# Weight tiles 64 bytes wider in a two-layer decoder trunk: six starts within 512 bytes

## The chip, the cores and the metric

The kernel runs on one core of a Trainium2 chip. The metric is the device time of one execution in microseconds (us). TensorE (PE in the profile; PEld is its weight load) multiplies matrices, VectorE (DVE), ScalarE (ACT) and GpSimd (POOL) do elementwise work, and SyncE (SP) issues nearly all DMA transfers.

## The reference

A sequence of 512 tokens with 1024 channels passes two layers in float32. Each layer is a mixer and a gated MLP, both with a residual sum and an RMSNorm ahead of them:

```
h = rmsnorm(x, norm_mix_e[e])
x = x + conv_mla_mixer(h, ...)      # layer 0: convolution branch + latent attention
h = rmsnorm(x, norm_mix_o[o])
x = x + pool_mixer(h, ...)          # layer 1: trailing means over 2, 4, 8, 16 tokens
...
h = rmsnorm(x, norm_ffn[l])         # both layers
uv = h @ w_up[l]                    # 1024 -> 2 x 2816
x = x + (silu(causal_dwconv(u)) * v) @ w_down[l]     # 2816 -> 1024
```

Layer 0's mixer projects h once; half of the columns go through a gated causal convolution of width 31 with a LayerNorm, the other part through attention with 8 heads and low-rank queries, keys and values. The output has a final RMSNorm. Nearly all arithmetic is in the projections, above all in the two MLPs.

## The kernel before

All activations are kept transposed: channels lie on the 128 partitions, the 512 tokens along the free dimension, in 8 tiles of 128 channels. A projection is a sum over such tiles, 128 channels at a time, into one bank of PSUM.

**Three matmuls for one product.** To keep float32 accuracy, each operand is split into a high and a low part of the type f32r, and a product is three matmuls: high x high, high x low and low x high. `mm3` (L107) issues them: L108 has the high weights and the high activations, L109 the high weights and the low activations, L110 the low weights and the high activations. The first operand of a matmul is the stationary one, which a weight load brings into TensorE; the second one streams past it. With few exceptions the weights are stationary, 128 x 128 at a time, and 512 tokens stream. In the profile's names the streaming operand comes first: `ps<-xgh,hi` streams the high activations against the high weights. The moving tiles are called xgh and xgl (inputs of a projection), gh and gl (the gated product in the MLP, bands and pooled values in the pooling mixer) and s (latents and attention). In two places the weights stream instead: the values of the attention (L580) and the pooling mixer's projection (L839).

**Weight tiles.** `stream` (L130) lists all weights in the order of their use, mostly in pieces of 128 x 1024, 4096 bytes on each partition. `fetch` (L146) brings one into a raw tile by a DMA that SP issues. `prepare` (L152) takes a high and a low tile and calls `split` (L96): ScalarE copies raw into hi (L97, rounding to f32r), VectorE writes raw - hi into lo (L98). `weights` (L164) hands the next pair out and prepares one ahead. There are three buffers each of raw, hi and lo, all from the pool `p_w`; a new hi waits until TensorE has done with the tile of three pieces ago. A weight tile holds eight blocks of 128 x 128, 512 bytes on a partition each, which `part` (L123) cuts out.

**Some matmuls are in plain f32**, of which the prediction speaks: 16 taps of the convolution (L392: 512 columns of u from offset j against a diagonal matrix), the scores (L511), the transposes (L546), probabilities times values (L558) and the sums of squares (L239). Each shows as two records in the profile.

**Where tiles lie.** Pools take their place one behind the other along the partition, consts, resid, `p_w`, `p_t` (temporaries), `p_s`, then the mixer's tiles or the MLP's gates from the left; the xg tiles lie at the far end, on the right side. Three unused tiles of `W_PAD`, `T_PAD` and `R_PAD` columns (4 bytes each) shift what follows them (L41, L143, L175, L273). The allocation of the built program gives these starts:

| tiles | start, bytes past a multiple of 512 |
|---|---|
| raw (3), hi (3), lo (3) | 0, each |
| xgh, xgl, gh, gl, s, u, q, keys, pt, v, tap | 0, each |
| t (8) | 96, 128, 160, 192, 224, 256, 288, 320 |
| sqr, rows, d | 352 |
| x, sq (ones, identity), causal | 320 |

Around the weight tiles no order is written by hand: each engine's instructions follow the program text, with waits where a tile's reader or writer is on another engine. The weight tiles' code is this, with what calls it:

Of the kernel before, what the change touches and what calls it, by code (L numbers as in the profile page):

```python
# [9 lines left out]
F32R = mybir.dt.float32r  # L10
# [5 lines left out]
P = 128  # L16
# [21 lines left out]

WARM = 40
PE_TAPS = 16  # L40
W_PAD, T_PAD, R_PAD = 48, 16, 120  # L41
GLU, LAT, BLK, END = 3, 4, 2, 0


# [1 line left out]
def kernel(  # L46
# [24 lines left out]
    p_w = ctx.enter_context(tc.tile_pool(name="weights", bufs=3))  # L71
# [7 lines left out]
    def uid(s):  # L79
        count[0] += 1  # L80
        return f"{s}{count[0]}"
# [14 lines left out]
    def split(dst, src):  # L96
        i = act.copy(dst[0], src)  # L97
        dve.tensor_tensor(dst[1], src, dst[0].bitcast(F32), op=ALU.subtract)  # L98
        return i
# [46 lines left out]
    def fetch():  # L146
        src, n = stream[len(raws)]
        raw = p_w.tile([P, 1024], F32, tag="raw", name=uid("raw"))[:, :n]
        nc.sync.dma_start(raw, src)
        raws.append(raw)  # L150

    def prepare():  # L152
        i = len(ready)
        if i == len(raws):
            fetch()
        n = stream[i][1]
        hi = p_w.tile([P, 1024], F32R, tag="hi", name=uid("hi"))[:, :n]
        lo = p_w.tile([P, 1024], F32R, tag="lo", name=uid("lo"))[:, :n]
        copied = split((hi, lo), raws[i])
        raws[i] = None  # L160
        ready.append((hi, lo))
        return copied

    def weights(ahead=1):  # L164
        given[0] += 1
        while len(ready) < min(given[0] + ahead, len(stream)):
            prepare()
        w = ready[given[0] - 1]
        ready[given[0] - 1] = None
        return w  # L170
# [112 lines left out]
    for k in range(KD):  # L283
        xk = p_x.tile([P, S], F32, tag="x", name=uid("x"))
        nc.sync.dma_start(xk, xT[k * P : (k + 1) * P, :])
        x.append(xk)
        fetch()
        if k < 3:
            opened = prepare()
        split_scaled(pair(xg[k]), xk, c(C_NE + k))  # L290
# [710 lines left out]
```

## Time and profile before

| | |
|---|---|
| median of 3 runs | 992.77 us (992.54 to 992.99) |
| the profiled execution | 993.86 us |
| its span, first to last instruction | 992.1 us |
| mean granted clock of TensorE | 0.991 |
| PE busy | 974.1 us (98%), 4476 matmuls |
| PEld busy | 799.2 us |
| DVE busy | 588.0 us |
| ACT busy | 402.4 us |
| POOL busy | 69.7 us |
| DMA | 91.99 MB, 27.3% of 16 engines' span on the main queue |

Busy time is a union: matmuls are pipelined, so that the next one starts before the one in front has ended, and a matmul's own duration (0.39 us for 512 columns) is longer than the interval from start to start. What a stream of matmuls costs is read from their starts. A group's row gives the line, engine, operation, tiles (out<-in) and count, then busy time and mean duration in ns, then the engine's idle time just before and what ended it. A row of waits gives the total in us, the number of waits and the longest. A row of the stretches gives the stretch, its length and for each engine busy time and count (PE, PEld, DVE, ACT, POOL), then the granted clock, the DMA engines' busy share and GB/s. The rows of DMA issues give count, size and the median time from issue to landing in us.

### The profile page before, as it was taken

The numbers are of one execution on the slowest core, as the hardware profiler recorded it, in microseconds if no ns is written. First come the engines' busy times: TensorE is split into PE (matmuls) and PEld (weight loads), VectorE is DVE, ScalarE is ACT, GpSimd is POOL, SyncE is SP. The second block draws the span as 40 slices with busy tenths as digits, with TensorE's granted clock in tenths as the row PEclk, the third lists the DMA queues.
The fourth block names the chain that finished last, engine by engine and source line by source line (L and its number), as shares of the span: only waits on it lengthen the run. The fifth ranks groups of instructions, "written<-read, shape, count | busy, mean of one in ns | idle before, by whom it ended". The sixth has DMA issues, their size and how long they took to land.

```text
span 992.1 us, 11547 instructions
## 1 busy us (share of the span) xinstructions
PE 974.1 (98%) x4476; PEld 799.2 (81%) x4476; DVE 588.0 (59%) x915; ACT 402.4 (41%) x582; POOL 69.7 (7%) x107
## 2 busy tenths in 40 slices
PE   8999999999999999999999999999999999999996
PEld 6888676777888888888888889888888888888885
DVE  4899989947575656565423338586656565522323
ACT  6435677534343333333222336253334333332321
POOL 5000100004000000000001102200000000000111
PEclk9999999989999999999999999999999999999998
DMA  6323101103233232323223241323232323223212
GB/s 219 127 89 112 39 22 44 64 29 105 100 107 106 85 106 85 106 85 107 91 101 106 85 159 44 107 86 101 90 104 88 106 85 107 93 98 105 86 43 85
DMA packets 29478, 91.99 MB, mean 93 GB/s; under 512 B 4080, under 2 KB 6384, under 8 KB 29424
## 3 DMA queue, kind: packets, MB, share of 16 engines
q1 hardware_dynamic: 28880, 90.74, 27.3%
q8 instruction: 35, 0.57, 0.2%
q10 hardware_dynamic: 544, 0.52, 0.2%
q14 instruction: 19, 0.16, 0.0%
HBM read 89.02 MB, written 2.23 MB: 92 GB/s over the span
## 4 chain that ended last, share of the span: by engine, by line
PE 94%; DVE 3%; DMA 1%; issue 1%; ACT 0%; SPq 0%; DVEq 0%; ACTq 0%
PE ps L108 28%; PE ps L110 28%; PE ps L109 28%; PE ps L511 2%; PE ps L558 2%; PE aux L392 1%; PE ps L546 1%; DVE lo L98 1%; PE aux L261 1%; DMA x<-in_xT_dram 1%; PE aux L239 1%; DVE xgl L103 0%; DMA col<-in_cols_dram 0%; PE ps L870 0%; PE ps L869 0%
## 5 line engine op out<-in xcount | busy, mean ns | idle before, releaser
L108 PE MATMUL ps<-xgh,hi 128*128 128x512 f32 x816 | 319.1, 391 | 2.8 <-ACT hi L97 2.8
L97 ACT CAST hi<-raw 128x1024 fp32r<-128x1024 f32 (+2 forms) x166 | 170.0, 1026 | 371.8 <-PE ps L109 344.3
L110 PE MATMUL ps<-xgh,lo 128*128 128x512 f32 x816 | 318.1, 391 | 1.1 <-DVE lo L98 1.0
L109 PE MATMUL ps<-xgl,hi 128*128 128x512 f32 x816 | 318.2, 390 | 0.0
L98 DVE TENSOR_TENSOR lo<-raw,hi 128x1024 fp32r<-128x1024 f32 (+2 forms) x166 | 201.2, 1214 | 156.8 <-ACT hi L97 156.2
L108 PEld LDWEIGHTS ps<-xgh,hi 128*128 128x128 f32 x816 | 153.6, 188 | 35.3 <-ACT hi L97 3.6
L110 PEld LDWEIGHTS ps<-xgh,lo 128*128 128x128 f32 x816 | 153.4, 188 | 35.0 <-DVE lo L98 3.1
L109 PEld LDWEIGHTS ps<-xgl,hi 128*128 128x128 f32 x816 | 153.6, 188 | 31.6
L108 PE MATMUL ps<-gh,hi 128*128 128x512 f32 (+1 forms) x374 | 141.1, 377 | 0.0
L109 PE MATMUL ps<-gl,hi 128*128 128x512 f32 (+1 forms) x374 | 140.9, 377 | 0.0
L110 PE MATMUL ps<-gh,lo 128*128 128x512 f32 (+1 forms) x374 | 140.8, 376 | 0.0
L110 PEld LDWEIGHTS ps<-gh,lo 128*128 128x128 f32 x374 | 70.4, 188 | 13.0
L108 PEld LDWEIGHTS ps<-gh,hi 128*128 128x128 f32 x374 | 70.4, 188 | 12.9
L109 PEld LDWEIGHTS ps<-gl,hi 128*128 128x128 f32 x374 | 70.4, 188 | 12.8
L698 DVE TENSOR_TENSOR t<-ps,rows 128x512 f32<-128x512 f32 x44 | 30.4, 691 | 77.2 <-PE ps L110 77.2
L226 POOL TENSOR_TENSOR sqr<-sqr,sqr 128x512 f32<-128x512 f32 x33 | 50.3, 1524 | 315.3 <-ACT sqr L224 285.3
L710 DVE TENSOR_TENSOR t<-ps,rows 128x512 f32<-128x512 f32 x44 | 30.4, 690 | 67.3 <-PE ps L110 67.1
L399 DVE SCALAR_TENSOR_TENSOR conv<-u,col,conv 128x512 f32<-128x512 f32 x90 | 67.4, 749 | 2.2 <-ACT conv L382 1.8
L705 DVE SCALAR_TENSOR_TENSOR t<-t,col,t 128x512 f32<-128x512 f32 x88 | 65.6, 748 | 1.4
L708 ACT ACTIVATE t<-t 128x512 f32<-128x512 f32 x44 | 27.8, 631 | 74.7 <-DVE t L705 74.7
L103 DVE SCALAR_TENSOR_TENSOR xgl<-x,col,xgh 128x512 fp32r<-128x512 f32 x32 | 32.7, 1037 | 13.2 <-ACT xgh L102 13.2
L108 PE MATMUL ps<-s,hi 128*128 128x512 f32 x96 | 39.5, 426 | 0.0
(182 smaller groups left out, 818.3 us busy)
## 6 DMA issues: line engine op xcount, KB each, us to landing
raw<-in_w_up_dram SPq DMA_DIRECT2D x88, 512.0 KB, 3.3
raw<-in_w_down_dram SPq DMA_DIRECT2D x44, 512.0 KB, 3.2
raw<-in_w_in_dram SPq DMA_DIRECT2D x10, 512.0 KB, 3.3
raw<-in_w_out_dram SPq DMA_DIRECT2D x8, 512.0 KB, 3.2
x<-in_xT_dram SPq DMA_DIRECT2D x8, 256.0 KB, 5.0
raw<-in_w_in_dram SPq DMA_DIRECT2D x8, 256.0 KB, 3.8
raw<-in_w_uq_dram SPq DMA_DIRECT2D x4, 384.0 KB, 3.1
raw<-in_w_ukv_dram SPq DMA_DIRECT2D x2, 512.0 KB, 4.2
```

The lines of the kernel that those rows point to most:

```text
L97: i = act.copy(dst[0], src)
L98: dve.tensor_tensor(dst[1], src, dst[0].bitcast(F32), op=ALU.subtract)
L103: dve.scalar_tensor_tensor(dst[1], src, scale, dst[0].bitcast(F32), op0=ALU.mult, op1=ALU.subtract)
L108: pe.matmul(ps, a[0], b[0], start=start, stop=False)
L109: pe.matmul(ps, a[0], b[1], start=False, stop=False)
L110: pe.matmul(ps, a[1], b[0], start=False, stop=stop)
L226: self.engine.tensor_tensor(self.parts[0], self.parts[0], t, op=ALU.add)
L399: i = dve.scalar_tensor_tensor(st["acc"], u[m][:, j : j + S], c(cw + j), st["acc"], op0=ALU.mult, op1=ALU.add,)
L698: dve.tensor_tensor(ut[:, 2 : 2 + S], pu, rows, op=ALU.mult)
L705: dve.scalar_tensor_tensor(a, ut[:, j : j + S], c(fw + j * NF + f), a, op0=ALU.mult, op1=ALU.add)
L708: act.activation(a, a, AF.Silu)
L710: dve.tensor_tensor(b, pv, rows, op=ALU.mult)
```

## The change

The high and low weight tiles become 1040 columns wide instead of 1024, of which the same 1024 are used, and the unused tile ahead of the weight pool's buffers grows from 48 to 80 columns.

```diff
-W_PAD, T_PAD, R_PAD = 48, 16, 120
+W_PAD, T_PAD, R_PAD = 80, 16, 120
...
-        hi = p_w.tile([P, 1024], F32R, tag="hi", name=uid("hi"))[:, :n]
-        lo = p_w.tile([P, 1024], F32R, tag="lo", name=uid("lo"))[:, :n]
+        hi = p_w.tile([P, 1040], F32R, tag="hi", name=uid("hi"))[:, :n]
+        lo = p_w.tile([P, 1040], F32R, tag="lo", name=uid("lo"))[:, :n]
```

The wider pad moves what follows it by 128 bytes, and each of the six wider tiles moves what follows it by 64 more, 512 in all. By the allocation of the built program the starts are now:

| tiles | start before | start after (bytes past a multiple of 512) |
|---|---|---|
| raw (3) | 0, 0, 0 | 128, 128, 128 |
| hi (3) | 0, 0, 0 | 128, 192, 256 |
| lo (3) | 0, 0, 0 | 320, 384, 448 |
| all others | as in the table above | the same |

The instructions of all five engines are the same in number, kind and order. In the steady state a block of weights, 512 bytes on a partition, was one aligned stretch of 512 bytes and now lies across two.

## The prediction

> **What bounds the kernel now.** I read the page first, then the busy time by stretch, then the waits of PE.
>
> ```profile
> PE 974.1 (98%) x4476; PEld 799.2 (81%) x4476; DVE 588.0 (59%) x915; ACT 402.4 (41%) x582; POOL 69.7 (7%) x107
> ...
> PE 94%; DVE 3%; DMA 1%; issue 1%; ACT 0%; SPq 0%; DVEq 0%; ACTq 0%
> ```
>
> PE is busy 98% of the span and makes up 94% of the chain that ended last. A busy PE need not be a PE at its peak, so the next view asks whether it ever stands still in the long stages.
>
> ```profile
> 250.00:580.00 330.00, 330.00 (x1464) 273.40 (x1463) 172.39 (x221) 115.57 (x140) 8.96 (x25) 1.00 0.29 97
> ```
>
> From 250 to 580 us (the first gated MLP) PE is busy for all 330 us at a granted clock of 1.00; DVE has 172 us of work there, ACT 116, the DMA engines 0.29 of their time. What PE waits for in the whole program is little, and of the weight tiles it waits for this:
>
> ```profile
> PE ps L108 <- ACT hi L97: 2.8, 2, 2.4
> ...
> PE ps L110 <- DVE lo L98: 1.0, 2, 0.8
> ```
>
> So the time is the number of matmuls times the interval from one matmul to the next. The timeline gives this interval (start, duration, engine), first for 512 columns, then (the last half of the last projection) for 256:
>
> ```profile
> 399.80 0.39 PE L108 MATMUL ps<-xgh,hi 128*128 128x512 f32 x1
> 400.03 0.39 PE L109 MATMUL ps<-xgl,hi 128*128 128x512 f32 x1
> 400.25 0.39 PE L110 MATMUL ps<-xgh,lo 128*128 128x512 f32 x1
> 400.26 0.19 PEld L108 LDWEIGHTS ps<-xgh,hi 128*128 128x128 f32 x1
> 400.48 0.39 PE L108 MATMUL ps<-xgh,hi 128*128 128x512 f32 x1
> ...
> 403.88 0.39 PE L108 MATMUL ps<-xgh,hi 128*128 128x512 f32 x1
> ```
> ```profile
> 969.90 0.28 PE L108 MATMUL ps<-gh,hi 128*128 128x256 f32 x1
> ...
> 970.98 0.28 PE L108 MATMUL ps<-gh,hi 128*128 128x256 f32 x1
> ```
>
> From 399.80 to 403.88 lie six triples, 18 matmuls: 4.08 us / 18 = 226.7 ns. From 969.90 to 970.98 lie nine: 120.0 ns. The difference, 106.7 ns for 256 columns, is 0.4167 ns a column; 512 columns take 213.3 ns, and a fixed part of 13.3 ns is left in each matmul. That fixed part is the one thing in the steady stream that could depend on where the weight tiles lie: the load for the next matmul (PEld, 400.26) begins with the running one (400.25) and takes less time than it.
>
> **The change, part by part.** No engine has an instruction more, fewer or in another place; only addresses move. In the allocation of the built program high, low and raw tiles all start at a multiple of 512 bytes before, as do the moving operands xg and g. After it the high tiles start at 128, 192 and 256 past such a multiple, the low ones at 320, 384 and 448, the raw ones at 128. Everything allocated behind them shifts by exactly 512.
>
> *TensorE, stationary operand.* These are the matmuls that load hi or lo as the stationary operand; each call of `mm3` issues one of each of L108, L109 and L110, so the rows of L108 stand for a third:
>
> ```profile
> L108 PE MATMUL ps<-xgh,hi 128*128 128x512 f32 x816 | 319.1, 391 | 2.8 <-ACT hi L97 2.8
> ...
> L108 PE MATMUL ps<-gh,hi 128*128 128x512 f32 (+1 forms) x374 | 141.1, 377 | 0.0
> ...
> L108 PE MATMUL ps<-s,hi 128*128 128x512 f32 x96 | 39.5, 426 | 0.0
> ```
>
> 3 x (816 + 374 + 96) = 3858. A block of 128 columns of 4 bytes is 512 bytes: before, each block is exactly one aligned stretch of 512 bytes, after, each straddles two, and its start is no longer at the same place within 512 as that of the operand that streams past. No matmul of this kind (f32r) in the trace has such addresses, so the cost must be bounded. The nearest rows are the matmuls in plain f32. Here are three pieces of the chain and three groups of weight loads:
>
> ```profile
> 112.27 0.86 PE aux L392 x2
> 113.13 1.50 PE ps L511 x4
> ...
> 127.09 2.16 PE ps L558 x8
> ```
> ```profile
> L108 PEld LDWEIGHTS ps<-xgh,hi 128*128 128x128 f32 x816 | 153.6, 188 | 35.3 <-ACT hi L97 3.6
> ...
> L511 PEld LDWEIGHTS ps<-keys,q 128*128 128x128 f32 x64 | 10.5, 190 | 6.4 <-issue 3.8 <-DVE s L514 0.2 <-ACT hi L97 0.2
> ...
> L239 PEld LDWEIGHTS aux<-sq,sqr 128*128 128x128 f32 x64 | 8.1, 191 | 0.4
> ```
>
> L392, a tap of the convolution, streams u from j x 4 bytes past a multiple of 512 (j from 0 to 15) against a stationary block at 0: 512 columns in 0.86 us. L511 has both operands at multiples of 512: 512 and 384 columns in 1.50 us, the same per column (1.68 ns and 1.67). Operands at the same place cost nothing that operands at different places don't. As to straddling: the square sums of L239 lie 352 bytes past a multiple, so their stationary blocks straddle it, and their loads take 191 ns against 190 for the aligned q of L511. Both ends are therefore near zero for f32. I take zero for f32r, whose load has the same length (188 ns) and ends some 30 ns before the next matmul starts (400.26 + 0.19 = 400.45 against 400.48).
>
> What the 13.3 ns are, the trace doesn't say, and this gives the two ends. In f32 the fixed part is smaller: L558 has 512 + 384 + 256 + 128 = 1280 columns, at four times 0.4167 ns 2133 ns, and took 2.16 us in 8 records, so 3.3 ns each. If the excess over that, 10.0 ns, comes from both operands lying at the same place within 512, the low end is -10.0 x 3858 = -38.6 us. If the 13.3 ns grow with the number of aligned 512-byte stretches that a block touches, the high end is +13.3 x 3858 = +51.3 us. I take the middle, because the f32 rows, the nearest, show neither. [...]
>
> *TensorE, moving operand.* The value projection of latent attention (24 matmuls of 512 columns, L580) and the pooling mixer (96 of 256, L839) stream hi and lo instead. By L392 a start off the 512 costs nothing; if each paid another 13.3 ns, 120 x 13.3 = 1.6 us.
>
> *ScalarE and VectorE.* 166 casts and 166 subtractions read and write the moved tiles. The 512-column forms show tiles at the same place beside tiles at different ones (t lies at 96 to 320 past a multiple):
>
> ```profile
> L97 ACT CAST gh<-t 128x512 fp32r<-128x512 f32 x44 | 27.3, 621 | 29.2 <-DVE t L711 29.2
> ...
> L97 ACT CAST hi<-raw 128x512 fp32r<-128x512 f32 x8 | 4.8, 615 | 2.9 <-PE ps L109 2.0 <-PE ps L110 0.9
> ```
> ```profile
> L98 DVE TENSOR_TENSOR gl<-t,gh 128x512 fp32r<-128x512 f32 x44 | 30.2, 686 | 1.4 <-ACT gh L97 1.4
> ```
> ```profile
> L98 DVE TENSOR_TENSOR lo<-raw,hi x166: 679/1224/2311, 5.6 to 962.8; 128x1024 fp32r<-128x1024 f32 x154, 128x512 fp32r<-128x512 f32 x8, 128x768 fp32r<-128x768 f32 x4
> ```
>
> 615 ns (all at 0) against 621 (mixed) on ScalarE; 679 (the fastest subtraction, a 512-column one) against 686 on VectorE. So at most 6 to 7 ns an instruction either way, 166 x 7 = 1.2 us of work on each engine, and almost all of it is covered:
>
> ```profile
> ACT hi L97 <- PE ps L109: 344.3, 130, 12.3
> ```
>
> ScalarE waits 344.3 us, in 130 places 2.6 us each, for PE to release a high tile. Of the 3.8 us that PE waits for both (rows above), four waits, a change of 7 ns moves 0.03 us. Were the cover gone, it would be the 1.2 us.
>
> *DMA.* The raw tiles go from a multiple of 256 bytes to 128 past one. The x tiles, which lie 64 past a multiple of 256, arrive at the start in turn with raw tiles of the same size:
>
> ```profile
> x<-in_xT_dram SPq DMA_DIRECT2D x3, 256.0 KB, 5.3
> raw<-in_w_in_dram SPq DMA_DIRECT2D x2, 256.0 KB, 5.3
> ```
>
> These are the issues from 2.1 to 4.4 us, alternating in one backlog: 5.3 us for either. So the cost is zero. The Trainium skill speaks against the change here ("DMA: Bandwidth & Descriptors", How a descriptor splits into AXI transactions): a piece that doesn't start at a multiple of 256 bytes needs a further transaction, 17 for a row of 4096 bytes where 16 did. By it every weight transfer would be about 6% longer; the two rows above don't show that, and 6% of the landing time below is 0.2 us, under the 2.6 us that ScalarE waits for each tile anyway.
>
> ```profile
> raw<-in_w_down_dram SPq DMA_DIRECT2D x44, 512.0 KB, 3.2
> ```
> ```profile
> SPq L149 <- DVE lo L98: 821.3, 153, 22.3
> ```
>
> The queue of SP waits for free raw tiles (821.3 us), so transfers have time in hand.
>
> **The sum.** 0 (stationary) + 0 (moving) + 0 (ACT, DVE, 0.03 at most) + 0 (DMA) = 0. The profiled execution took 993.86 us, 992.1 of span and 1.8 around it; it is 1.1 us above the median of 992.77 of the runs shown. With no term I forecast 992.8 us. A measurement of this kernel tells about 0.2% from no change, 2.0 us, so 990.8 to 994.8 counts as the same. In terms of the stream 2.0 us are 2.0 / 3858 = 0.5 ns a matmul: a quarter of a percent of the interval would already be seen.
>
> **The rivals.**
>
> *Faster: the common start was a collision.* Before, every stationary block and every moving block of the f32r matmuls starts at the same place within 512 bytes, and the load begins with the matmul that it runs beside. If they then meet in the same part of the memory, the 10.0 ns over the f32 form are what it costs, and the change removes up to 38.6 us: 954.2 us. For it: the excess is there in every one of these matmuls, at 512 and 256 columns alike. Against it: L511, with equal starts, pays nothing over L392. The skill's measured back-to-back interval for 512 columns of bf16 ("TensorE: Matmul & The Clock Gate", Part 1) is 215.7 ns, by which, as an estimate, the stream could lose 11.0 x 3858 = 42.4 us; no run here shows a bf16 matmul of that size.
>
> *Slower: a straddling weight block costs a second start.* The 13.3 ns are the part of a load that can't lie beside the running matmul, one start for each aligned 512 bytes; every block now touches two. Place: all 3858 loads; price up to 51.3 us: 1044.1 us. It decides from 0.5 ns a matmul on. For it: the trace has no straddling f32r load that would exclude it. Against it: the f32 loads of L239 straddle at 191 ns, and a load may grow by some 30 ns before the interval must follow.
>
> *The change does nothing to the addresses.* The allocation of the built program shows them moved, so this has no chance of its own.
>
> **How the numbers follow.** No change: 0.64. Faster: 0.17. Slower: 0.19, a little more, since a straddling block is new to this program in f32r, while equal starts were there in f32 and cost nothing. The time is that of the likeliest case, 992.8. Each rival may apply to part of the blocks or of the price, so I spread it evenly from 2 us to its end. A range from 974 to 1014 then holds all of the first case, (18.8 - 2) / 36.6 = 0.46 of the second and (21.2 - 2) / 49.3 = 0.39 of the third: 0.64 + 0.08 + 0.07 = 0.79.
>
> **What would show it.** Right: in the same stretch from 250 to 580 us PE is full again and three matmuls start every 0.68 us; weight loads stay at 188 ns, and the waits of PE for hi and lo stay under 4 us. Faster would show as fewer than 226.7 ns from start to start, slower as more, with or without longer loads; were the intervals unequal among the six buffers, the place within 512 bytes would matter by itself. The forecast is wrong if the interval moves by more than 0.5 ns, or if idle time of PE, before ps <- ACT hi or DVE lo, grows by more than 2 us.

## The result, and the profile after

The changed kernel takes 1009.06 us (median of 4 runs, 1007.76 to 1009.52) against 992.78 us: a ratio of 1.0162, interval 1.0144 to 1.018. It is slower by 16.3 us. The profiled execution took 1009.52 us with a span of 1007.6.

The page has the same engines in the same roles:

```profile
PE 989.8 (98%) x4476; PEld 799.6 (79%) x4476; DVE 588.3 (58%) x915; ACT 402.0 (40%) x582; POOL 69.7 (7%) x107
...
PE 94%; DVE 3%; DMA 1%; issue 1%; SPq 0%; ACT 0%; DVEq 0%; ACTq 0%
```

PE is busy 15.7 us longer (989.8 - 974.1), the span is 15.5 us longer, and the work of the others has not grown. In the first MLP the stretch from 250 to 580 us shows it:

```profile
250.00:580.00 330.00, 330.00 (x1435) 268.46 (x1434) 170.89 (x219) 113.35 (x138) 8.97 (x25) 1.00 0.29 96
```

PE is full as before and its clock 1.00, but 1435 matmuls fit in instead of 1464, 2.0% fewer: an interval of 226.7 x 1464 / 1435 = 231.3 ns instead of 226.7. The timeline of PE shows what became of the steady beat:

```profile
300.41 0.39 PE L108 MATMUL ps<-xgh,hi 128*128 128x512 f32 x1
300.63 0.39 PE L109 MATMUL ps<-xgl,hi 128*128 128x512 f32 x1
300.87 0.39 PE L110 MATMUL ps<-xgh,lo 128*128 128x512 f32 x1
301.09 0.39 PE L108 MATMUL ps<-xgh,hi 128*128 128x512 f32 x1
301.32 0.39 PE L109 MATMUL ps<-xgl,hi 128*128 128x512 f32 x1
301.54 0.40 PE L110 MATMUL ps<-xgh,lo 128*128 128x512 f32 x1
301.78 0.39 PE L108 MATMUL ps<-xgh,hi 128*128 128x512 f32 x1
```

From start to start now lie 220 to 240 ns, changing from one matmul to the next. The intervals are also unequal among the three buffers, which the prediction named as the sign that the place within 512 bytes matters by itself: by the starts in the trace, the mean interval of one weight tile (24 matmuls) runs through 230.0, 232.9 and 230.8 ns, tile after tile through the first MLP, in the order of the three buffers. What could have hidden behind another name didn't move. The weight load is as long as before within 1 ns, PE waits for the weight tiles as it did (2.9 us for the high ones, 2.8 before), the subtractions take what they took, and x and raw tiles still arrive alike at the start, no later than before (six rows of four views: groups, waits, the tile lo, DMA from 2.1 to 4.4 us):

```profile
L108 PEld LDWEIGHTS ps<-xgh,hi 128*128 128x128 f32 x816 | 154.1, 189 | 38.5 <-ACT hi L97 3.5
...
L108 PEld LDWEIGHTS ps<-gh,hi 128*128 128x128 f32 x374 | 70.4, 188 | 14.4
```
```profile
PE ps L108 <- ACT hi L97: 2.9, 2, 2.5
```
```profile
L98 DVE TENSOR_TENSOR lo<-raw,hi x166: 679/1224/2318, 5.4 to 978.9; 128x1024 fp32r<-128x1024 f32 x154, 128x512 fp32r<-128x512 f32 x8, 128x768 fp32r<-128x768 f32 x4
```
```profile
x<-in_xT_dram SPq DMA_DIRECT2D x3, 256.0 KB, 4.7
raw<-in_w_in_dram SPq DMA_DIRECT2D x2, 256.0 KB, 4.7
```

The f32r matmuls with 512 columns and weights as the stationary operand number 3 x (816 + 330 + 96) = 3726; the 330 are the 374 less the 44 with 256 columns. At 226.7 ns each, 2.0% of them are 17 us: within what one matmul more or less in the count allows, the whole loss.

### The profile page after: what moved, and what is told of

Read it like the earlier page. It is cut to its first block, busy times and chain, and to the rows that moved or that the text cites. A ratio compares the mean times of both kernels' runs of the same rounds, so it can differ in the third digit from the quotient of the medians.

```text
span 1007.6 us, 11547 instructions
## 1 busy us (share of the span) xinstructions
PE 989.8 (98%) x4476; PEld 799.6 (79%) x4476; DVE 588.3 (58%) x915; ACT 402.0 (40%) x582; POOL 69.7 (7%) x107
## 4 chain that ended last, share of the span: by engine, by line
PE 94%; DVE 3%; DMA 1%; issue 1%; SPq 0%; ACT 0%; DVEq 0%; ACTq 0%
PE ps L108 29%; PE ps L110 28%; PE ps L109 28%; PE ps L511 2%; PE ps L558 2%; PE aux L392 1%; PE ps L546 1%; DVE lo L98 1%; PE aux L261 1%; PE aux L239 1%; DMA x<-in_xT_dram 1%; DVE xgl L103 0%; DMA col<-in_cols_dram 0%; PE ps L870 0%; PE ps L869 0%
## 5 line engine op out<-in xcount | busy, mean ns | idle before, releaser
L108 PE MATMUL ps<-xgh,hi 128*128 128x512 f32 x816 | 322.5, 395 | 2.9 <-ACT hi L97 2.9
L110 PE MATMUL ps<-xgh,lo 128*128 128x512 f32 x816 | 321.5, 395 | 0.9 <-DVE lo L98 0.8
L109 PE MATMUL ps<-xgl,hi 128*128 128x512 f32 x816 | 321.8, 394 | 0.0
```

Of the source, the lines that this page charges most:

```text
L108: pe.matmul(ps, a[0], b[0], start=start, stop=False)
L109: pe.matmul(ps, a[0], b[1], start=False, stop=False)
L110: pe.matmul(ps, a[1], b[0], start=False, stop=stop)
```

## The experiments

The theories: (1) the difference between the starts of the stationary and of the streaming block counts; (2) a stationary block that straddles a multiple of 512 bytes costs; (3) the engines and transfers that work on the moved tiles slow PE down; later (4) a start that changes from matmul to matmul is bad, and any steady one is good. The ratios below are to runs of the kernel before that were taken together with the run in question (medians of 992.43 and 992.55 us).

**PE alone, one start at a time.** A kernel without any of the layers: stationary blocks in tiles of 136 columns, each 32 bytes further past a multiple of 512 than the last, streaming blocks in tiles of 528 columns, 64 bytes further each.

```diff
+    def stretch(name, a, b, n=64):
...
+        for k in range(n):
+            pe.matmul(ps, a, b, start=k == 0, stop=k == n - 1)
```

> This kernel computes none of the layers; its output is a copy of x and one product. It runs stretches of 64 f32r matmuls (512 columns, one new weight load each) with PE alone at work: first the stationary block from 0 to 480 bytes past a multiple of 512 in steps of 32 with the moving block at 0, then 4, 8 and 16 bytes past; then the moving block from 64 to 448 with the stationary one at 0; then both at the same 64 to 448; then one in bf16; then the order high, high, low of the changed kernel's three buffers. Theory 1 (what counts is the difference of the two starts): 226.7 ns from start to start wherever both starts are equal, other intervals, 228 to 236 ns, wherever they differ, in the first set as in the second, and about 230, 232 and 231 ns in the order of the three buffers. Theory 2 (what counts is that the stationary block straddles a multiple of 512): 226.7 ns whenever it lies at 0, so in the whole second set, and about 231 ns at every other start, equal starts included. Theory 3 (the slower interval comes from ScalarE, VectorE or DMA working on the moved tiles beside PE): 226.7 ns in every stretch. bf16: near 216 ns if the 13.3 ns belong to f32r, 226.7 if to any matmul of 512 columns.

The groups of PE (stationary tiles sa to sp at 0 to 480, streaming ones ma at 0, mb at 64):

```profile
L112 PE MATMUL pa<-ma,sd 128*128 128x512 f32 x64 | 15.1, 396 | 0.0
...
L112 PE MATMUL pa<-ma,se 128*128 128x512 f32 x64 | 15.0, 395 | 0.0
...
L112 PE MATMUL pa<-ma,sg 128*128 128x512 f32 x64 | 14.8, 392 | 0.0
...
L112 PE MATMUL pe<-mb,sa 128*128 128x512 f32 x64 | 14.8, 391 | 0.0
L112 PE MATMUL pf<-mb,sc 128*128 128x512 f32 x64 | 14.7, 390 | 0.0
...
L112 PE MATMUL pa<-ma,si 128*128 128x512 f32 x64 | 14.7, 389 | 0.0
...
L112 PE MATMUL pg<-bm,bs 128*128 128x512 bf16 x62 | 13.9, 379 | 0.1
```

A stretch's busy time is 63 intervals and one matmul: 15.1 us is (15.1 - 0.4) / 63 = 233 ns, 14.7 is 227. From the starts in the trace, in ns (mean of the last 48 intervals of a stretch; for a difference of 0 the last stretch of the run):

| stationary past streaming, bytes | 0 | 32 | 64 | 96 | 128 | 160 | 192 | 224 |
|---|---|---|---|---|---|---|---|---|
| 0 to 224 | 226.7 | 233.3 | 233.3 | 234.3 | 232.4 | 233.3 | 228.9 | 233.3 |
| 256 to 480 | 226.7 | 233.3 | 233.3 | 234.3 | 232.4 | 233.3 | 228.9 | 233.3 |

The curve repeats after 256 bytes. Moving the streaming block by 64 instead (mb with sa: a difference of -64, or 192) gives 228.9, as 192 does; equal starts at 64 (mb with sc), and at every other place tried, give 226.7. So straddling (2) is out, writers and DMA (3) aren't needed, and for one steady start (1) holds, modulo 256. bf16 took 215 to 216 ns. In the order high, high, low of the changed kernel's three buffers the trace gave 229.9, 234.2 and 231.3 ns, 231.8 on the mean, against 230.0, 232.9 and 230.8 in the kernel; two rows of the first of them, six triples apart, (517.56 - 513.42) / 18 = 230 ns:

```profile
513.42 0.63 PE L128 MATMUL pi<-ma,se 128*128 128x512 f32 x2
...
517.56 0.63 PE L128 MATMUL pi<-ma,se 128*128 128x512 f32 x2
```

**All starts moved alike, in the kernel.** Weights, xg, gates and latents all at 128.

```diff
-W_PAD, T_PAD, R_PAD = 48, 16, 120
+W_PAD, T_PAD, R_PAD = 80, 16, 216
```

> Weight tiles and everything that streams (xg, gates, latents) all start 128 bytes past a multiple of 512, widths as before. Theory 1 (difference of starts): 992.8 us within 0.2%, every interval 226.7 ns. Theory 2 (straddling): every stationary block straddles, so about 1009 us. Theory 3 (writers and DMA on tiles off the multiple): also slower than before, about 1009 us.

992.97 us, ratio 1.0005 (0.9996 to 1.0015), with 1465 matmuls in the same stretch:

```profile
250.00:580.00 330.00, 330.00 (x1465) 273.48 (x1464) 173.35 (x222) 114.82 (x141) 8.98 (x25) 1.00 0.28 96
```

Every weight block straddles here, and the raw, high and low tiles lie where the change put raw: no cost.

**Weights at 256, the rest at 0.**

```diff
-W_PAD, T_PAD, R_PAD = 48, 16, 120
+W_PAD, T_PAD, R_PAD = 112, 80, 120
```

> Raw, high and low tiles all start 256 bytes past a multiple of 512, everything else as before. Theory 1: one fixed difference of 256 between the starts, so one steady interval or one short repeating pattern in the whole kernel, between 224 and 236 ns, 985 to 1030 us. Theory 2: every block straddles, 231 ns, 1009 us, as with six different starts. Theory 3: about 1009 us.

992.87 us, ratio 1.0004 (0.9995 to 1.0013). A difference of 256 counts as none, as in the stretches. A straddling block costs nothing here either.

**The raw tiles alone.** A second pad behind the raw buffers puts high and low back on multiples of 512.

```diff
-W_PAD, T_PAD, R_PAD = 48, 16, 120
+W_PAD, T_PAD, R_PAD = 80, 16, 120
...
+        if not raws:
+            p_w.tile([P, 96], F32, tag="pad2", bufs=1, name="w_pad2")
```

> Only the raw tiles start 128 bytes past a multiple of 512, as after the change; high and low tiles are at multiples of 512, as before. Theories 1 and 2: 992.8 us within 0.2%. Theory 3: a good part of the 16.3 us, so 1000 to 1009 us.

992.83 us, ratio 1.0007 (0.9997 to 1.0016): DMA targets, and what ScalarE and VectorE read, cost nothing. (3) is out in the kernel too.

**High at 0, low at 256.** After the result with 256, a steady difference of any size might have been harmless (theory 4). Here the starts differ from one matmul to the next.

```diff
-W_PAD, T_PAD, R_PAD = 48, 16, 120
+W_PAD, T_PAD, R_PAD = 48, 80, 120
...
+        if not ready:
+            p_w.tile([P, 64], F32, tag="pad2", bufs=1, name="w_pad2")
         lo = p_w.tile(...)
```

> Raw and high tiles at multiples of 512 as before, the low tiles 256 bytes past one; all else as before. Theory 1a (difference modulo 256): no change, 992.4 us within 0.2%. Theory 4 (starts that differ from one matmul to the next): slower, on two of three matmuls, 1000 us or more.

992.94 us, ratio 1.0001 (0.9992 to 1.0011): different starts aren't bad by themselves.

**Weights all at 128, and all at 192.** The other half of that question, and a test of the curve's size.

```diff
-W_PAD, T_PAD, R_PAD = 48, 16, 120
+W_PAD, T_PAD, R_PAD = 80, 112, 120      # 128
+W_PAD, T_PAD, R_PAD = 96, 96, 120       # 192
```

> Raw, high and low tiles all 128 bytes past a multiple of 512, all else as before. Theory 1a: the 232.4 ns that the single stretches showed for a difference of 128, so 3726 matmuls of 512 columns x 5.7 ns = 21 us, 1014 us; slower than the change itself. Theory 4: one steady difference as with 256, 992.4 us.

> Raw, high and low tiles all 192 bytes past a multiple of 512, all else as before. Theory 1a: 228.9 ns as in the single stretches, 3726 x 2.2 ns = 8 us, 1001 us. Theory 4: 992.4 us. Were only the distance from the multiple of 256 to count, whatever its sign, 192 would lie as far from it as 64 and take 233.3 ns, 1017 us.

At 128: 1012.07 us, ratio 1.02 (1.0185 to 1.0216), against 1014 expected by (1). At 192: 1000.3 us, ratio 1.0077 (1.006 to 1.0094), against 1001. With the one fixed start of 128, and no spread at all, the kernel is slower than with the change. The same stretch, 128 first:

```profile
250.00:580.00 330.00, 330.00 (x1429) 267.80 (x1428) 170.90 (x219) 113.39 (x138) 9.02 (x25) 1.00 0.27 94
```
```profile
250.00:580.00 330.00, 330.00 (x1450) 271.00 (x1449) 172.11 (x220) 114.53 (x139) 9.02 (x25) 1.00 0.27 96
```

1464 / 1429 and 1464 / 1450 times 226.7 are 232.3 and 228.9 ns: the 232.4 and 228.9 of PE alone. Theory 4 falls.

**Is there a better start?** Finer steps and pairs, as first, first, second.

```diff
+    for i in range(8):
+        for j in range(8):
+            ps = stretch("p" + letter(i) + letter(j), (32 * i, 32 * i, 32 * j))
```

> Again no layer is computed. Stretches of 45 f32r matmuls of 512 columns, the streaming block always at a multiple of 512. First a single stationary start: 4 to 28 bytes in steps of 4, the odd multiples of 16 from 48 to 240, and 244, 248, 252. Then the order first, first, second as in the kernel's triples, with both from 0 to 224 in steps of 32 (64 pairs). Theory 1a (the difference of the starts modulo 256 bytes counts): 226.7 ns for the pair 0, 0 and 228 to 235 ns elsewhere, a triple's mean near the mean of the three single intervals; no stretch under 226. Theory 4 (any steady pattern is good, changing starts are bad): the pairs with equal starts at 226.7, the unequal ones above. Open in both: whether some start or pair comes under 226.7 ns, toward the 215.7 of bf16.

No. The fine starts gave 228.3 to 235.0 ns, but for 252 bytes, four before the next multiple of 256, with 226.7. Of the 64 pairs 0, 0 is the best with 226.7; next come 228.9 (four pairs with the first at 192), the worst is 235.6. Two things came out other than expected. A triple isn't near the mean of its single intervals: 0, 0, 32 took 233.3 ns, as much as 32 alone, where that mean is 228.9; 37 of the 64 pairs lie 1 ns or more from it, up to 4.4. And 192, 192, 128 took 231.1 ns, where the second buffer's order above, 192, 192, 384, took 234.2: alike modulo 256, but not alike in time (the orders of the other two buffers came out as above, 230.0 and 231.1). So with starts that alternate the difference modulo 256 doesn't give the interval by itself, and why isn't shown. Two rows, the fine starts of 112 and 252; 46 matmuls touch either stretch, of 10.45 and 10.15 us:

```profile
120.90:131.35 10.45, 10.45 (x46) 8.38 (x45) 0.00 (x0) 0.00 (x0) 0.00 (x0) 1.00 0.00 0
193.95:204.10 10.15, 10.15 (x46) 8.41 (x45) 0.00 (x0) 0.00 (x0) 0.00 (x0) 1.00 0.00 0
```

So the kernel before already has the best layout that was found, and none of the versions tried is faster.

**Which streaming block, and which types?**

```diff
+    for i, d in enumerate((32, 64, 128, 192)):
+        stretch("own" + letter(i), (at(0), at(d)), (mat(0), mat(d)))
+        stretch("run" + letter(i), (at(0), at(d)), (mat(d), mat(0)))
```

> No layer is computed. Theory 1a says the start of a stationary block against that of the streaming block decides, but not which streaming block: that of its own matmul (1a-own) or that of the matmul that runs while the block is loaded (1a-running). Stretches named own alternate two matmuls whose own blocks start alike (0 with 0, d with d; d = 32, 64, 128, 192), so that each load runs beside a block that starts d away; stretches named run alternate 0 with d and d with 0, so that each load runs beside a block that starts alike. 1a-own: own 226.7 ns, run 228 to 234 ns. 1a-running: own 228 to 234 ns, run 226.7 ns. Then bf16 (half) with the stationary block 0, 32, 64, 96, 128, 192 bytes off: 215.7 ns at 0, and the same everywhere if the start counts for f32r alone. Then f32 (full), the same starts: two records of 429 ns each, the same everywhere by what taps and scores showed before the change. Then f32r with 256 columns (short), at 0, 32, 64, 128, 192: 120.0 ns at 0; in the changed kernel such matmuls fell to 112 to 122 ns, so 116 to 121 off the zero.

Both theories missed: own gave 231.7, 231.7, 228.3 and 231.7 ns, run 230.0, 233.3, 230.0 and 233.3 (d = 32, 64, 128, 192). Neither a matmul whose own blocks start alike nor a load beside a stream that starts alike is enough when the streaming start alternates. The types are clear: bf16 took 215.8 ns and f32 429 ns a record at all six starts. With 256 columns f32r took 120.0 ns at equal starts and 117.8 to 118.6 at the others.

```profile
L122 PE MATMUL shorta<-mv,q 128*128 128x256 f32 x48 | 6.3, 291 | 0.0
...
L122 PE MATMUL shortc<-mv,q 128*128 128x256 f32 x48 | 5.8, 281 | 0.0
```

**Smaller loads.**

```diff
+                pe.matmul(ps[:n, :], part(d, n), mat(0), ...)     # n = 128, 96, 64, 32
```

> No layer is computed. Stretches of 48 f32r matmuls of 512 columns whose stationary block has 128, 96, 64 or 32 columns (ca, cb, cc, cd), starting 0, 32, 64, 128 and 192 bytes past the streaming block's multiple of 512. Collision (the reads of the weight load and of the stream get into each other's way): the excess over the 215.8 ns of bf16 shrinks with the columns loaded, from 10.9 ns at 128 to about 3 ns at 32 with equal starts, and from 17.5 ns (233.3) to about 5 ns at 32 with a start 32 or 64 off. Fixed length (the 13.3 ns are a part of every f32r matmul or load that lies bare): at equal starts about the same interval for 96 and 128 columns or a fall in proportion to the columns, and the loss at other starts stays the same 6 to 7 ns for all sizes. Then streams of 384, 256 and 128 columns with full blocks at 0, 64, 128 off: at 256 as measured 120.0, 117.8, 118 ns; a collision gives 384 columns an excess between those of 256 and 512.

In ns by the start of the block, as the mean of the last 36 intervals of a stretch:

| columns loaded | 0 | 32 | 64 | 128 | 192 |
|---|---|---|---|---|---|
| 128 | 226.7 | 233.3 | 233.3 | 232.4 | 228.9 |
| 96 | 230.0 | 228.9 | 228.3 | 226.7 | 233.3 |
| 64 | 230.0 | 231.7 | 232.6 | 229.3 | 228.3 |
| 32 | 231.6 | 240.0 | 231.7 | 230.6 | 231.7 |

Both readings missed again. A quarter of the load isn't cheaper, so the loss isn't bytes that collide with bytes; and it isn't fixed either. With 96 columns, 384 bytes, the good start moves to 128, where the block ends at a multiple of 256, as the 128-column block does from 0; with 64 and 32 columns no such start stands out. With full blocks and a shorter stream, 384 columns show the loss as well (173.3, 176.7 and 176.0 ns at 0, 64 and 128), 256 gave 120.0, 117.8 and 118.6 again, and 128 gave 111.7 at all three. The rows of 384, at 64, 128 and 0:

```profile
L122 PE MATMUL wab<-mv,q 128*128 128x384 f32 x48 | 8.6, 338 | 0.0
L122 PE MATMUL wac<-mv,q 128*128 128x384 f32 x48 | 8.6, 338 | 0.0
L122 PE MATMUL waa<-mv,q 128*128 128x384 f32 x48 | 8.5, 334 | 0.0
```

## Why the prediction was right or wrong

**What bounds the kernel: right.** The stream of matmuls sets the time, and the loss is all in its interval; 0.5 ns a matmul was named as the point of decision, and it moved by 4.6.

**The step that failed** is the stationary operand: "I take zero for f32r", by the rows of plain f32. The range held the result, and that was luck: no change was the forecast and the likeliest case, and neither came; the upper part of the range was the reach of a rival, straddling, that cost nothing. Those rows were right for f32 and say nothing for f32r: f32 is as fast at all six starts in the stretches, and f32r isn't. The nearest row was near in everything but the data type that mattered. The term that was put at zero measured 16 to 17 us, 4.6 ns a matmul, between the two ends of -38.6 and +51.3 us.

**The rivals.** The sign was that of the slower rival, which had 0.19, but not its mechanism: straddling blocks cost nothing at 256 in the kernel and nothing at equal starts anywhere. The point that a load ends some 30 ns before the next matmul was no shelter: the loads stayed at 188 to 189 ns and the interval grew all the same. The faster rival had the right quantity, the difference of the two starts, and the wrong sign: the common start is the best of those tried, not a collision.

**The 13.3 ns** aren't one fixed length: the measured interval moves between 226.7 and 235 ns with the address alone, and with 256 columns it falls below 120.0. What they are stays open. The bf16 interval of 215.7 ns that the Trainium skill gives ("TensorE: Matmul & The Clock Gate", Part 1) agrees with the 215 to 216 here.

**The terms at zero: right.** ScalarE, VectorE and DMA: raw alone at 128 cost nothing (ratio 1.0007, interval across 1), the groups kept their durations. The further transaction that the Trainium skill gives a piece off a multiple of 256 bytes ("DMA: Bandwidth & Descriptors", How a descriptor splits into AXI transactions) doesn't show for these writes: with raw alone at 128 the weights of the MLP landed in 3.2 us, as with raw at 256. That section tells of bytes that are fetched, and here only the written side moved. The moving operand of L580 and L839, bounded at 1.6 us, wasn't tried by itself; in the changed kernel the matmuls of L839 start 117 to 119 ns apart, 120 before, so it cost nothing there.

**What stays open** is how. That the loss needs f32r (bf16 and f32 showed none at six starts), that with one steady start it goes by the difference of the starts modulo 256 bytes, and that it is there with PE alone is shown. Which two accesses get in each other's way isn't: neither pairing of load and stream explained the alternating starts, and the size of the load didn't scale it. That the intervals in a stretch repeat in short cycles, 226 to 232 ns at 192, reads as if the start of each load slides against the stream, but that is only argued.

## What to carry to other kernels

With f32r matmuls that load a new block of 128 columns each time and stream 512, give stationary and streaming tiles starts that are equal modulo 256 bytes, and check it in the allocation: weight tiles widened by 64 bytes, behind a pad widened by 128, cost 1.6% here with the same instructions in the same order. For other sizes measure it, since blocks of 96 columns and streams of 256 had other best starts. Read the interval from start to start, or count matmuls in a fixed stretch; a PE at 98% busy, loads at 188 to 189 ns and nearly unchanged waits showed nothing of it. A row of another data type is no bound for the one at hand: a microkernel of the type at hand, with PE alone, gave the mean interval in the kernel within 0.5 ns.

## What the runs showed of the hardware that wasn't expected

With one steady start and blocks of 128 columns, the interval of f32r with 512 columns goes by the start difference modulo 256, between 226.7 and 235.0 ns, and 252 bytes is as good as 0. With 256 columns it goes the other way: 120.0 ns at equal starts, 117.8 to 118.7 at others. The last projection of the changed kernel shows that too; its 256-column matmuls start 117 ns apart on the mean, waits left out, and by the two rows its fastest 13 took 1.49 us, 115 ns each:

```profile
985.48 0.28 PE L110 MATMUL ps<-gh,lo 128*128 128x256 f32 x1
...
986.97 0.28 PE L108 MATMUL ps<-gh,hi 128*128 128x256 f32 x1
```
